# First modulation blocks loaded together; four column blocks of FFN 1 in plain products

## The chip, the cores and the metric

The kernel runs on 1 core of a Trainium2 chip. The metric is device time in microseconds for one execution. Engines are named as the profile names them: PE (TensorE matmul), PEld (its weight load), DVE (VectorE), ACT (ScalarE), POOL (GpSimd) and SP (SyncE, which issues the DMAs here).

## The reference

One layer, D = 1024, 512 latent tokens (`x`) and 256 context tokens (`xc`). Cut to what the change touches:

```
x = x + grid_pos_embedding
m  = split(silu(c)     @ w_mod + b_mod, 9)      # modulation of the latents
mc = split(silu(c_ctx) @ w_mod + b_mod, 9)      # of the context
h  = rmsnorm(x, g_n1) * (1 + m[1]) + m[0]
x  = x  + 0.5 * m[2]  * swiglu(h,  w_ffn1_up, w_ffn1_down)     # FFN 1, hidden 2816
xc = xc + 0.5 * mc[2] * swiglu(hc, w_ffn1_up, w_ffn1_down)
...                                                            # mixers on rmsnorm(x), rmsnorm(xc)
x  = x + m[5] * (merged @ w_out)
x  = x + 0.5 * m[8] * swiglu(mod(rmsnorm(x)), w_ffn2_up, w_ffn2_down)
y  = rmsnorm(x, g_final)
swiglu(x): g, u = split(x @ w_up); (silu(g) * u) @ w_down
```

## The kernel before

Features lie on the partitions: `x` is 8 feature blocks of 128 x 512, `xc` 8 of 128 x 256. Every f32 operand and weight is split into a high part (ACT, `split`, L146) and a low part (DVE, L147), and each product takes three matmuls: high weight by high operand, high by low, low by high. A Tile scheduler fixes each engine's order at build time.

**Start.** `mod_first(k)` (L198) makes m[0] and m[1] of feature block k: it loads 1 MB of weights through the rotating `raw` buffers (4 of 128x1024, `wload`, L149), runs 8 matmuls of 256 columns (L203), transposes the result on DVE (L206) and adds the bias in 8 small additions (L211). Blocks 0 to 4 stand ahead of the norm, blocks 5 to 7 inside `hook1`, between the norm and the FFN. The norm sums squares of `x` and `xc` (ACT L277, DVE L279), two matmuls with ones add them up (L283), and the reciprocal roots `rs` and `rsc` follow on ACT and DVE (L303 to L309). Each feature block is then scaled on DVE (`xr`, L617 and L618) and modulated on ACT (L632).

**FFN 1** runs over 22 column blocks of w_up (each 128 gate columns with their 128 up columns), in groups of 4, 4, 4, 4, 2, 4; after each group the matching rows of w_down are applied (L173 to L177 with operand `H`, then L560 and L562 into `x` and `xc`). The 768 tokens are cut into two halves of 384 columns and the 8 feature blocks into pairs. An up block is computed by seven block products in place of eight (`UpBlock`, `product`, L425 to L427): 7 x 4 x 3 = 84 matmuls of 384 columns. For that, DVE forms sums of weights (`UpWeights.b`, L393 to L398) and, once, sums of operands (`Operands.sums`, L356 to L359), and afterwards combines the products (L466 to L483). Four products need sums of operands. Three pairs of split weights are buffered (`whi`, `wlo`, WB = 3).

**Beside it** `more_mods` computes the other modulation parts on DVE, two products with 128x1024 weights per step (L234); m[2] has to be there when the first w_down is applied.

**The output projection** (`run_parts`, 8 blocks of w_out, first over tokens 0 to 255, then over 256 to 511) loads and splits each block of w_out in both passes.

Of the kernel before, what the change touches and what calls it, by code (L numbers as in the profile page):

```python
# [48 lines left out]
GRID_W = 64  # L49
UW = 2 + CTX + 4 + SEQ + 1  # L50
# [17 lines left out]
def block_kernel(ctx: ExitStack, tc: tile.TileContext, io):  # L68
# [110 lines left out]
    def both(t, k):  # L179
        return [t[0][:, k], t[1][:, k]]  # L180
# [4 lines left out]
    nhs, nls = (nhc, nh), (nlc, nl)  # L185
# [11 lines left out]

    def mod_first(k):  # L198
        ps = psum_small()
        raw = wload(io["wmod01"][k], 2048)  # L200
        last["mod"] = last["load"]
        for i in range(KB):
            T.matmul(ps[:, :256], c32[:, i, :], raw[i // 4][:, (i % 4) * 256:(i % 4 + 1) * 256],  # L203
                     start=(i == 0), stop=(i == KB - 1))
        tt = A.tile([P, 256], F32, name="tt", bufs=2)
        V.transpose(tt, ps[:, :256])  # L206
        tv = tt.rearrange("p (B q r) -> p B q r", B=2, q=4)
        for q in range(4):
# [9 lines left out]
    M[0], M[1] = mod_tile(0), mod_tile(1)  # L218
# [107 lines left out]
    class Operands:  # L326
# [36 lines left out]
        WHERE = {1: ("b1", 0), 2: ("b2", 0), 3: ("b2", 1), 4: ("tb", 1), 5: ("tb", 0), 6: ("ta", 0), 7: ("ta", 1)}  # L363

# [121 lines left out]
    def ffn(reg, up, downs, gate, two, ops, begin, parts, between):  # L486
# [3 lines left out]
        sel = (lambda t, k: [t[:, k, :CTX], t[:, k, CTX:]]) if two else (lambda t, k: [t[:, k]])  # L490
        x = X[0]
        groups = GROUPS[two]
        ahead = 1 if two else 2
        ws = [UpWeights(reg, up[f]) for f in range(FB)]
        f0 = 0
        blocks_ = [UpBlock(u, ops) for u in ws]
        for f in range(ahead):
            ws[f].a()
# [17 lines left out]
        for gi, gs in enumerate(groups):  # L516
            hs = reg[0].tile([P, 2 * HMAX[two] * w], F32R, name="H")
            hh, hl = (hs[:, i * HMAX[two] * w:(i * HMAX[two] + gs) * w].rearrange("p (k n) -> p k n", k=gs)
                      for i in range(2))
            for i in range(gs):  # L520
                f = f0 + i
                if i < gs - 1:
                    ws[f + 1].load()
# [6 lines left out]
                split(u, hh[:, i], hl[:, i])  # L530
# [21 lines left out]
            if gi < len(groups) - 1:  # L552
                for d in range(KB):
# [4 lines left out]
                    for k in range(gs):  # L558
                        mm(ps, wt, k, sel(hh, k), sel(hl, k), k == 0, k == gs - 1)
# [4 lines left out]
            else:  # L564
                between(100)
                run_parts(parts, weights if two else weights_held, gs, lambda k, c: (hh[:, k, c], hl[:, k, c]), g)
# [48 lines left out]
    xr = A.tile([P, KB * ALL], F32, name="xr", tag="H").rearrange("p (k n) -> p k n", k=KB)  # L615
    for k in range(KB):
# [8 lines left out]
    def hook1():  # L625
        for k in range(KB):
            if k > 4:
                mod_first(k)
# [470 lines left out]
```

## Time and profile before

| | |
|---|---|
| median of 3 runs | 1515.37 us (1514.85 to 1519.92) |
| the profiled execution's own time | 1515.29 us |
| its span | 1513.5 us |
| mean granted TensorE clock | 0.983 |
| PE, DVE, ACT busy | 94%, 84%, 48% of the span |

Read the profile by stretches: the shares of the whole span hide that the first 70 us differ from all that follows. A row of a timeline gives start, duration, engine, line, operation, output and input; brackets give the idle time ahead and what ended it. Times of PE's single matmuls overlap, so the distance of two starts is the pace, not the duration.

### The profile page before, as it was taken

To read this page: it belongs to the slowest core of one execution; us is meant where nothing else is said; L and a number is where in the kernel's file an instruction comes from. 1 tells how busy PE (TensorE), PEld (TensorE's weight loads), DVE (VectorE), ACT (ScalarE), POOL (GpSimd) and SP (SyncE) were. 2 spreads that over 40 slices of the span, in tenths; PEclk is the share of its full clock that TensorE was granted. 3 is DMA by queue.
4 is the path that set the end of the run, shared out by engine and by line. 5 is a ranking of instruction groups with operands and counts; after the bars stand their busy time and mean duration, and the time that the engine had idled before them with its cause. 6 is when DMAs were issued, how large, how long until landed. Compare 5 with 4: busy or idle time off the path is not lost.

```text
span 1513.5 us, 20675 instructions
## 1 busy us (share of the span) xinstructions
PE 1429.8 (94%) x8094; PEld 1280.4 (85%) x8094; DVE 1265.9 (84%) x1957; ACT 730.6 (48%) x1011; POOL 11.4 (1%) x55
## 2 busy tenths in 40 slices
PE   6599999999999999999999989999996999999997
PEld 5498898989988997787788768778896989999897
DVE  6998998876768868999999999966589968678686
ACT  4642341423313345578888862246366525435252
POOL 0000000000000000000000020000000000000000
PEclk9899999999999999999999999999997999999998
DMA  7435444351425134222222223233351333333331
GB/s 283 139 114 171 153 147 150 118 185 55 159 93 181 57 98 147 77 67 74 75 72 91 71 63 94 80 112 141 109 169 56 98 112 98 99 99 96 112 98 56
DMA packets 49346, 169.02 MB, mean 112 GB/s; under 512 B 5600, under 2 KB 7904, under 8 KB 48608
## 3 DMA queue, kind: packets, MB, share of 16 engines
q1 hardware_dynamic: 49248, 167.70, 34.2%
q8 instruction: 63, 1.03, 0.3%
q14 instruction: 35, 0.29, 0.1%
HBM read 163.48 MB, written 4.19 MB: 111 GB/s over the span
## 4 chain that ended last, share of the span: by engine, by line
PE 63%; DVE 24%; DMA 7%; issue 3%; ACT 3%; DVEq 0%; SPq 0%; ACTq 0%
PE psm L177 11%; PE psm L175 11%; PE psm L173 11%; PE psm L425 9%; PE psm L426 8%; PE psm L427 8%; DVE wlo L147 5%; DMA raw<-in_wmod 4%; DVE cv L742 3%; DMA raw<-in_down 2%; ACT whi L146 1%; PE psm L203 1%; DVE raw L234 1%; PE ps L175 1%; PE ps L173 1%
## 5 line engine op out<-in xcount | busy, mean ns | idle before, releaser
L146 ACT ACTIVATE whi<-raw 128x1024 fp32r<-128x1024 f32 (+2 forms) x230 | 233.2, 1014 | 356.7 <-PE psm L175 235.9
L147 DVE TENSOR_TENSOR wlo<-raw,whi 128x1024 fp32r<-128x1024 f32 (+2 forms) x230 | 267.5, 1164 | 38.7 <-ACT whi L146 38.4
L742 DVE SCALAR_TENSOR_TENSOR cv<-u,vec,cv 128x512 f32<-128x512 f32 x236 | 165.2, 743 | 0.5
L173 PE MATMUL psm<-H,whi 128*128 128x256 f32 (+1 forms) x496 | 151.2, 354 | 4.2 <-ACT H L146 4.2
L175 PE MATMUL psm<-H,whi 128*128 128x256 f32 (+1 forms) x496 | 151.4, 353 | 0.0
L177 PE MATMUL psm<-H,wlo 128*128 128x256 f32 (+1 forms) x496 | 150.6, 352 | 0.0
L173 PE MATMUL psm<-nh,whi 128*128 128x512 f32 x336 | 133.0, 398 | 6.9 <-ACT u L724 2.8
L177 PE MATMUL psm<-nh,wlo 128*128 128x512 f32 x336 | 132.6, 395 | 3.6 <-DVE wlo L147 3.6
L175 PE MATMUL psm<-nl,whi 128*128 128x512 f32 x336 | 133.0, 396 | 1.7 <-DVE nl L317 1.5
L425 PE MATMUL psm<-nbx,whi 128*128 128x384 f32 x286 | 97.6, 342 | 14.6 <-ACT nbx L146 8.2
L173 PEld LDWEIGHTS psm<-H,whi 128*128 128x128 f32 x496 | 92.5, 188 | 18.4 <-ACT H L146 5.7
L175 PEld LDWEIGHTS psm<-H,whi 128*128 128x128 f32 x496 | 92.9, 188 | 13.7 <-DVE H L147 0.7
L177 PEld LDWEIGHTS psm<-H,wlo 128*128 128x128 f32 x496 | 93.2, 188 | 12.9
L426 PE MATMUL psm<-nbx,whi 128*128 128x384 f32 x286 | 97.2, 340 | 0.9 <-DVE nbx L147 0.9
L427 PE MATMUL psm<-nbx,wlo 128*128 128x384 f32 x286 | 96.5, 340 | 0.4 <-DVE wlo L147 0.3
L425 PE MATMUL psm<-nb,whi 128*128 128x256 f32 x264 | 77.3, 294 | 10.1 <-ACT nb L146 9.2
L234 DVE SCALAR_TENSOR_TENSOR raw<-raw,cb 128x1024 f32<-128x1024 f32 x56 | 68.2, 1219 | 18.2 <-DMA raw<-in_wmod 18.1
L173 PEld LDWEIGHTS psm<-nh,whi 128*128 128x128 f32 x336 | 63.9, 191 | 21.6 <-ACT u L724 3.1
L426 PE MATMUL psm<-nl,whi 128*128 128x256 f32 (+1 forms) x264 | 79.9, 303 | 0.0
L560 DVE SCALAR_TENSOR_TENSOR x<-psm,m,x 128x512 f32<-128x512 f32 x64 | 47.8, 746 | 38.4 <-PE psm L177 38.4
L146 ACT ACTIVATE whi<-s 128x1024 fp32r<-128x1024 f32 x44 | 46.7, 1062 | 68.0 <-PE psm L426 24.5
L177 PEld LDWEIGHTS psm<-nh,wlo 128*128 128x128 f32 x336 | 64.0, 191 | 18.1 <-DVE wlo L147 4.6
(296 smaller groups left out, 3772.9 us busy)
## 6 DMA issues: line engine op xcount, KB each, us to landing
raw<-in_up SPq DMA_DIRECT2D x88, 512.0 KB, 3.8
raw<-in_wmod SPq DMA_DIRECT2D x72, 512.0 KB, 4.1
raw<-in_down SPq DMA_DIRECT2D x30, 512.0 KB, 4.0
raw<-in_down SPq DMA_DIRECT2D x24, 384.0 KB, 3.3
raw<-in_wvg SPq DMA_DIRECT2D x16, 512.0 KB, 3.8
raw<-in_wout SPq DMA_DIRECT2D x16, 512.0 KB, 4.0
raw<-in_wlx SPq DMA_DIRECT2D x10, 512.0 KB, 3.8
raw<-in_wlg SPq DMA_DIRECT2D x10, 512.0 KB, 3.7
```

The source lines that it names most:

```text
L146: S.activation(hi, src, AF.Copy)
L147: V.tensor_tensor(lo, src, f32(hi), op=ALU.subtract)
L173: T.matmul(p_, hi[:, wk, :], h, start=first, stop=False)
L175: T.matmul(p_, hi[:, wk, :], l, start=False, stop=False)
L177: T.matmul(p_, lo[:, wk, :], h, start=False, stop=last)
L203: T.matmul(ps[:, :256], c32[:, i, :], raw[i // 4][:, (i % 4) * 256:(i % 4 + 1) * 256], start=(i == 0), stop=(i == KB - 1))
L234: V.scalar_tensor_tensor(o, raw, 1.0, cb[j], op0=ALU.mult, op1=ALU.mult, accum_out=out[:, j:j + 1])
L425: T.matmul(ps, hi[:, o + k, :], h, start=first and k == 0, stop=False, **kw)
L426: T.matmul(ps, hi[:, o + k, :], l, start=False, stop=False, **kw)
L427: T.matmul(ps, lo[:, o + k, :], h, start=False, stop=k == 3, **kw)
L560: V.scalar_tensor_tensor(x[:, d], ps[-1], g[:, d, 0:1], x[:, d], op0=ALU.mult, op1=ALU.add)
L742: V.scalar_tensor_tensor(o, u[:, t:t + SEQ], wdw[:, j, t:t + 1], o, op0=ALU.mult, op1=ALU.add)
```

## The change

- The 8 MB of weights of `mod_first` get space of their own, in tiles that hold later operands (`nh`, `nbx`, two context tiles). All loads are issued at once, among those of `x` and `xc`; five matmul groups run ahead of the norm's end, three inside `hook1`. The bias is added for both parts in one instruction (4 in place of 8 per block).
- The weights of the first two up blocks are loaded early, too.
- The first group of FFN 1 (4 up blocks) is computed in eight plain block products (`PlainBlock`): 8 x 4 x 3 = 96 matmuls of 384 columns per block, no sums of weights, no combinations afterwards. Its first block goes by feature block: as soon as feature block k is split, its 12 matmuls are issued. The sums of operands that later groups need are made one pair per plain block (`sums1`).
- `H` is four tiles in place of one.
- In the output projection the split weights of blocks 3 to 7 are kept for the second pass (40 KB per partition), so that it loads and splits three in place of eight.

```
+    def mod_load(k, dst):
+        at[k] = dst
+        for a in range(0, 2048, 1024):
+            last["mod"] = nc.sync.dma_start(dst[:, a:a + 1024], io["wmod01"][k][:, a:a + 1024])
...
     def mod_first(k):
         ps = psum_small()
-        raw = wload(io["wmod01"][k], 2048)
...
+            T.matmul(ps[:, :256], c32[:, i, :], at[k][:, i * 256:(i + 1) * 256], start=(i == 0), stop=(i == KB - 1))
...
+    class PlainBlock:
...
+        def step(self, kk, start, stop):
+            if self.ps is None:
+                self.ps = [[psum_small()[:, :self.nw] for _ in range(2)] for _ in range(2)]
+            i, half = kk // 2, kk % 2
+            b = [self.ops.plain(half, c, i) for c in range(2)]
+            for wt, ps in zip(self.wt, self.ps):
+                mm(ps, wt, kk, [h for h, _ in b], [l for _, l in b], start, stop, wk=half * 4 + i)
...
         if two:
-            begin()
-            ws[0].b()
-            ws[0].c()
-            ws[0].d()
+            for p_ in plain[:2]:
+                p_.load()
+            plain[0].prepare()
+            begin(lambda kk: plain[0].step(kk, kk == 0, kk == KB - 1))
...
+                if f < len(plain):
+                    if f + 1 < len(plain):
+                        plain[f + 1].prepare()
...
+                    if f:
+                        plain[f].all()
+                    u = plain[f].post()
+                    sums(f)
...
-    mod_first(0)
+    mod_load(0, spare[0])
+    mod_load(1, spare[1])
     nc.sync.dma_start(pos, io["pos"])
     nc.sync.dma_start(x[:, :4], io["x"][:, :4])
-    mod_first(1)
     nc.sync.dma_start(x[:, 4:], io["x"][:, 4:])
+    mod_load(2, spare[2])
     nc.sync.dma_start(xc, io["xc"])
-    for k in range(2, 5):
+    first_up = [UpWeights([A], io["up1"][f]) for f in range(2)]
+    for k in range(3, KB):
+        mod_load(k, spare[k])
+        if k in (4, 7):
+            first_up[k == 7].load()
+    for k in range(MA):
         mod_first(k)
...
+    def hook1(step):
...
         for k in range(KB):
-            if k > 4:
-                mod_first(k)
+            if k + MA < KB:
+                mod_first(k + MA)
+            if k + 1 < KB:
+                scale_x(k + 1)
...
+            step(k)
...
+    def out_weights(d, key):
+        if d in held:
+            return held[d]
```

SP, from its start: before, each line with `raw` waits for a free one of the four buffers.

```order
L154 DMA raw<-in_wmod 128x1024 x2
L595 DMA pos<-in_pos 128x288
L596 DMA x<-in_x 128x2048
L154 DMA raw<-in_wmod 128x1024 x2
L598 DMA x<-in_x 128x2048
L599 DMA xc<-in_xc 128x2048
L154 DMA raw<-in_wmod 128x1024 x6
L154 DMA raw<-in_up 128x1024 x2
L154 DMA raw<-in_wmod 128x1024 x6
```

SP, the same place after; `mod` is the new space, which nothing holds yet.

```order
L204 DMA mod_72<-in_wmod 128x1024 x4
L666 DMA pos<-in_pos 128x288
L667 DMA x<-in_x 128x2048
L668 DMA x<-in_x 128x2048
L204 DMA mod_101<-in_wmod 128x1024 x2
L670 DMA xc<-in_xc 128x2048
L204 DMA mod_101<-in_wmod 128x1024 x4
L158 DMA raw<-in_up 128x1024 x2
L204 DMA mod_101<-in_wmod 128x1024 x2
L204 DMA mod_77<-in_wmod 128x1024 x2
L204 DMA mod_78<-in_wmod 128x1024 x2
L158 DMA raw<-in_up 128x1024 x2
```

Both halves of `x` and one more modulation block now stand ahead of `xc`, and all eight modulation blocks are issued without a wait.

PE, from its start, before (`psm<-raw` are the modulation matmuls, L425 to L427 the first products of FFN 1):

```order
L203 MATMUL psm<-raw,c_95 128x256 x33
L283 MATMUL psm<-acc,ones 128x512
L283 MATMUL psm<-accc,ones 128x256
L203 MATMUL psm<-raw,c_95 128x256 x27
L425 MATMUL psm<-nhc,whi 128x384
L203 MATMUL psm<-raw,c_95 128x256 x4
L426 MATMUL psm<-nlc,whi 128x384
L427 MATMUL psm<-nhc,wlo 128x384
```

PE after, the same place (L177 to L181 are the plain products, `nl` and `p` their operands of feature block 0):

```order
L209 MATMUL psm<-mod_72,c_95 128x256 x16
L209 MATMUL psm<-mod_101,c_95 128x256 x22
L290 MATMUL psm<-acc,ones 128x512
L290 MATMUL psm<-accc,ones 128x256
L209 MATMUL psm<-mod_101,c_95 128x256 x10
L177 MATMUL psm<-nl,whi 128x384
L177 MATMUL psm<-p_299,whi 128x384
L177 MATMUL psm<-nl,whi 128x384
L177 MATMUL psm<-p_299,whi 128x384
L209 MATMUL psm<-mod_77,c_95 128x256 x2
L179 MATMUL psm<-nl,whi 128x384
L181 MATMUL psm<-nl,wlo 128x384
```

The first FFN product now follows 48 modulation matmuls in place of 60 and is followed by further products of the same feature block. From the second w_down stage of FFN 1 up to the output projection, and from FFN 2's first products to the end, the instructions of PE and DVE stand in the same order before and after, but for two matmuls that change places.

## Rows read from the trace of the kernel before

**Rows 1.** Stretches: length, then busy us (count) by engine, PE clock, DMA share, GB/s.
```profile
0.00:6.00 6.00, 0.16 (x1) 0.20 (x2) 1.11 (x2) 1.50 (x2) 0.48 (x7) 1.00 0.61 174
6.00:21.00 15.00, 11.39 (x42) 9.34 (x43) 10.21 (x34) 4.55 (x10) 0.16 (x2) 1.00 1.02 417
...
51.00:66.00 15.00, 4.41 (x15) 2.54 (x13) 13.82 (x46) 11.98 (x18) 0.00 (x0) 0.73 0.25 82
...
68.50:128.50 60.00, 58.75 (x320) 57.27 (x321) 56.16 (x85) 23.72 (x35) 0.00 (x0) 0.97 0.39 126
128.50:163.20 34.70, 33.86 (x194) 29.57 (x193) 31.31 (x56) 7.15 (x9) 0.00 (x0) 1.00 0.50 161
```

**Rows 2.** Chain of waits: start, us, what; the last modulation block.
```profile
49.80 2.01 PE psm L203 x8
```

**Rows 3.** PE's timeline: two paces, w_down of the first group, the next up block.
```profile
68.98 0.52 PE L425 MATMUL psm<-nbx,whi 128*128 128x384 f32 x1
69.30 0.52 PE L426 MATMUL psm<-nbx,whi 128*128 128x384 f32 x1
...
75.10 0.33 PE L425 MATMUL psm<-nl,whi 128*128 128x384 f32 x1
75.27 0.33 PE L426 MATMUL psm<-nl,whi 128*128 128x384 f32 x1
...
128.59 0.51 PE L173 MATMUL psm<-H,whi 128*128 128x256 f32 x2
...
163.23 0.33 PE L425 MATMUL psm<-nhc,whi 128*128 128x384 f32 x1
...
167.58 0.44 PE L425 MATMUL psm<-nbx,whi 128*128 128x384 f32 x1 [2.10 <-ACT whi L146]
```

**Rows 4.** DVE's groups, 0 to 70 us: count, busy us, mean ns, idle ahead.
```profile
L147 DVE TENSOR_TENSOR nh<-xr,nh 128x768 fp32r<-128x768 f32 x2 | 1.9, 952 | 0.0
L147 DVE TENSOR_TENSOR nbx<-xr,nbx 128x384 fp32r<-128x384 f32 x3 | 1.7, 554 | 0.3 <-ACT nbx L146 0.3
...
L393 DVE TENSOR_TENSOR s<-raw 128x512 f32<-128x512 f32 x1 | 0.7, 691 | 1.7 <-DMA raw<-in_up 1.7
```

**Rows 5.** ACT's groups, 0 to 70 us, in the same columns.
```profile
L632 ACT ACTIVATE xr<-xr,m,G 128x512 f32<-128x512 f32 x8 | 6.4, 802 | 3.4 <-DVE xr L617 3.4
L632 ACT ACTIVATE xr<-xr,m,G 128x256 f32<-128x256 f32 x8 | 4.7, 592 | 3.0 <-DVE G L263 2.4 <-DVE xr L618 0.5
...
L146 ACT ACTIVATE nbx<-t 128x768 fp32r<-128x768 f32 x5 | 4.2, 835 | 0.5 <-DVE t L359 0.5
...
L228 ACT ACTIVATE cb<-cb 128x1024 f32<-128x1024 f32 x2 | 2.1, 1058 | 1.5 <-DMA cb<-in_cc 1.5
...
L146 ACT ACTIVATE nbx<-xr 128x384 fp32r<-128x384 f32 x3 | 1.5, 508 | 0.0
...
L228 ACT ACT_TABLE_LOAD x1 | 1.3, 1283 | 0.0
```

**Rows 6.** Timeline of DVE and ACT around the norm and the first scaled feature blocks.
```profile
17.45 0.42 ACT L275 ACTIVATE accc<-xc 128x256 f32<-128x256 f32 x1 [5.52 <-DMA xc<-in_xc]
...
33.67 0.65 DVE L617 TENSOR_TENSOR xr<-x,rs 128x512 f32<-128x512 f32 x1
...
36.27 0.52 ACT L146 ACTIVATE nhc<-xr 128x384 fp32r<-128x384 f32 x1
...
37.40 0.68 DVE L617 TENSOR_TENSOR xr<-x,rs 128x512 f32<-128x512 f32 x1
38.00 0.42 DVE L618 TENSOR_TENSOR xr<-xc,rsc 128x256 f32<-128x256 f32 x1
```

**Rows 7.** DVE's groups, 68.5 to 128.5 us, in the columns of Rows 4.
```profile
L147 DVE TENSOR_TENSOR wlo<-raw,whi 128x1024 fp32r<-128x1024 f32 x8 | 9.8, 1221 | 2.5 <-ACT whi L146 2.5
```

**Rows 8.** Stretches late in the run, in the columns of Rows 1.
```profile
1120.00:1130.00 10.00, 10.00 (x85) 10.00 (x84) 10.00 (x22) 9.82 (x22) 0.00 (x0) 1.00 0.49 166
...
1150.00:1160.00 10.00, 8.30 (x29) 6.82 (x30) 9.37 (x21) 6.45 (x12) 0.00 (x0) 0.50 0.13 45
```

More of the change, by code (lines that the diff above doesn't have):

```diff
@@ L363, in block_kernel, with plain @@
         WHERE = {1: ("b1", 0), 2: ("b2", 0), 3: ("b2", 1), 4: ("tb", 1), 5: ("tb", 0), 6: ("ta", 0), 7: ("ta", 1)}
+        def plain(self, half, c, k):
+            tag, o = (("b1", 0), ("b12", 0), ("b2", 0), ("b2", 1))[half * 2 + c]
+            return [t[:, o * self.nw:(o + 1) * self.nw] for t in self.parts[tag, k]]
         def of(self, p, k):
@@ L484, in rest, with __init__, load, prepare @@
             return u
-    def ffn(reg, up, downs, gate, two, ops, begin, parts, between):
+    class PlainBlock:
+        def __init__(self, w, ops):
+            self.w, self.ops, self.nw, self.ps = w, ops, ops.nw, None
+        def load(self):
+            self.w.load()
+        def prepare(self):
+            self.load()
+            self.wt = [self.w.pair(r) for r in self.w.raw]
+        def step(self, kk, start, stop):
[5 more added lines that the diff above has]
+                mm(ps, wt, kk, [h for h, _ in b], [l for _, l in b], start, stop, wk=half * 4 + i)
+        def all(self):
+            order = [2 * i + h for h in range(2) for i in range(4)]
+            for kk in order:
+                self.step(kk, kk == order[0], kk == order[-1])
+        def post(self):
+            nw = self.nw
+            g, u = tmp(2 * nw), tmp(2 * nw)
+            for c in range(2):
+                o = slice(c * nw, c * nw + nw)
+                S.activation(g[:, o], self.ps[0][c], AF.Silu)
+            for c in range(2):
+                o = slice(c * nw, c * nw + nw)
+                V.tensor_tensor(u[:, o], self.ps[1][c], g[:, o], op=ALU.mult)
+            return u
@@ L489, in ffn @@
+    def ffn(reg, up, downs, gate, two, ops, begin, parts, between, sums=None):
         w = ALL if two else SEQ
-        sel = (lambda t, k: [t[:, k, :CTX], t[:, k, CTX:]]) if two else (lambda t, k: [t[:, k]])
+        sel = (lambda t: [t[:, :CTX], t[:, CTX:]]) if two else (lambda t: [t])
         x = X[0]
         groups = GROUPS[two]
-        ahead = 1 if two else 2
-        ws = [UpWeights(reg, up[f]) for f in range(FB)]
+        ahead = 0 if two else 2
+        ws = (first_up if two else []) + [UpWeights(reg, up[f]) for f in range(2 if two else 0, FB)]
@@ L565, in ffn @@
                 between(100)
[L566 removed]
+                run_parts(parts, weights if two else weights_held, gs, lambda k, c, hs=hs: (hs[k][:, 0, c], hs[k][:, 1, c]), g)
             f0 += gs
@@ L621, in block_kernel, with scale_x @@
+    def scale_x(k):
+        V.tensor_tensor(xr[k][:, CTX:], x[:, k], rs1, op=ALU.mult)
+        V.tensor_tensor(xr[k][:, :CTX], xc[:, k], rs1c, op=ALU.mult)
+    scale_x(0)
     flat = "p k n -> p (k n)"
     ops1 = Operands(ALL // 2)
-    ops1.place([t.rearrange(flat) for t in (nh, nl, nhc, nlc)] + [nbx], b2=2, ta=2, tb=2, b1=1)
-    def hook1():
+    tiles = {}
+    def hook1(step):
+        plain = Operands(ALL // 2)
+        plain.add([A.tile([P, 1024], F32R, name="p21", tag="s21"), A.tile([P, 512], F32R, name="p4", tag="s4")]
+                  + [A.tile([P, 512], F32R, name=f"p4{t}", tag=f"w4{t}") for t in "hl"]
+                  + [keep("acc", SEQ, F32R), keep("rs", SEQ, F32R), A.tile([P, 384], F32R, name="p0")])
+        plain.place(b12=1)
+        ops1.parts.update(plain.parts)
+        nw = ALL // 2
```

109 lines of the change are left out of this document (73 added, 36 removed).

## The prediction

> **What bounds the kernel now.** I read the busy time by stretches first, then PE's own timeline, then the groups of DVE and ACT in the first 70 us. From 68.5 us on PE is the engine that sets the pace: in the 60 us of the first four up blocks it is busy for 58.75 us, in the following w_down stage for 33.86 of 34.70 us [rows 1]. DVE is close behind (56.16 and 31.31 us), so a change there has to keep both in view. Before 68.5 us PE has little to do: between 51 and 66 us it is busy for 4.41 of 15 us, at a mean granted clock of 0.73 [rows 1]. Two things hold it up there, one after the other. The modulation blocks come through four buffers, so the last is multiplied only at 49.80 us and is done at 51.81 [rows 2], although the transfers ran at 417 GB/s between 6 and 21 us [rows 1]. Then DVE and ACT split the operands and their sums, and only when these are nearly through do the seven-product blocks run without gaps. The marks of the run before: 68.5 us (dense matmuls begin; 16 of the first block's 84 are through), 128.59 (first w_down), 163.23 (next up block) [rows 3].
>
> **The loads.** The 417 GB/s were reached with several transfers in flight [rows 1]; I take that rate for the new order, in which nothing waits for a buffer, and that data land in the order of issue. By 6 us 1.04 MB are in (174 GB/s [rows 1]), and so come: `x` complete (4.4 MB) at 14 us, `xc` (6.5 MB) at 19.1, modulation block 4 (8.6 MB) at 24, the first up weights at 26.6, modulation block 7 (12.8 MB) at 34, the second up weights at 36.7. So modulation leaves the path: by the DVE sum below its turn comes at about 48 us. `xc` comes 1.65 us later than the 17.45 of before [rows 6], since a modulation block stands ahead of it now. Against that, DVE stood for 1.7 us on the first up weights in the middle of the root chain [rows 4]; these now land before it. I set the two off: first `xr` at 33.7 us as before, first split operand at 36.8 us as before [rows 6]. Bounds: 1.7 us either way.
>
> *A rule weighed.* The Trainium skill (DMA: Bandwidth & Descriptors, Bandwidth) sets reads from device memory at about 358 GB/s per core; the trace differs with its 417 GB/s, and the measurement decides here. By the page `xc` would land some 2 us later, and the sum would be 2 us longer.
>
> **The first block, by feature block.** Three engines work side by side from 34 to 60 us, and the last of them decides. Neighbouring instructions of DVE overlap by 0.08 us (a 0.68 us addition is followed after 0.60) [rows 6]; I take that off on DVE and 0.1 us on ACT.
> - DVE: eight `xr` pairs at 0.94 us, 7.5 [rows 6]; low parts, eight of 384 columns at 0.47 and four of 768 at 0.87, 7.2 [rows 4]; two weight splits at 1.14 and one modulation product, taken as long as a split of its width, 3.4 [rows 7]; three transposes and twelve small bias additions, 2.5 by estimate from the 0.42 us of a 256-wide addition [rows 6]. Sum 20.6, from 33.7: 54.3 us.
> - ACT: eight modulated blocks at 0.70 + 0.49, 9.5; high parts, eight at 0.41 and four at 0.74, 6.2; three operations of 1024 columns at 0.96, 2.9; one table load, 1.3 [rows 5]. Sum 19.9, from 34.4: 54.3 us.
> - Each hands over to the other some ten times. Their groups stood between 0 and 3.4 us for such waits [rows 4, 5]; I add 2.5 in all (0 to 6). Last low part 57 us, and with the rest of the last feature block's matmuls 59 us.
> - PE: 96 matmuls at 0.174 (75.10 to 75.27 [rows 3]), 16.7; two modulation blocks at 2.01 [rows 2], 4.0; from 36.8: 57.5 us. PE stands for about 5 us before this, and the dense work of before began at the lower clock after its gaps: 0.32 us per matmul from 68.98 to 69.30, 0.174 at 75.10 [rows 3], so up to 6 us at half pace. I take 5 us, 2.5 us lost (0 to 3): 60.0 us.
>
> So block 1 of the group can begin at **60 us** (57 to 65).
>
> **The other three plain blocks.** 3 x 96 x 0.174 = 50.1 us. Per block this is 2.1 us more PE time than the 84 matmuls of before; it is what the change pays. DVE's work per block is two weight splits (2.3), two multiplications out of PSUM (0.9), one pair's sums (1.9 + 1.7), one low part of `H` (0.9) and four modulation products (4.6, by their width again): 12.3 us [rows 4, 7], under PE's 16.7. The two weight splits are the narrow place: with three buffers the second pair of the next block can only be split when the block before has read its first pair for the last time. From there PE has 12 matmuls (2.1 us) to the first use of the new high part and 16 (2.8 us) to its low part; ACT and DVE need 1.06 and 1.22 us [rows 5, 7], together 2.3. It fits if DVE is free at that moment, and costs up to 1.1 us where a modulation product is in front. I take 1.0 us in all (0 to 7). First w_down at 60 + 50.1 + 1 = **111.1 us**, 17.5 before the 128.59 of now.
>
> **w_down and the next up block.** The 192 matmuls of w_down are the same, 34.6 us (163.23 - 128.59): next up block at 145.7. There PE waited 2.10 us for split weights, which come from DVE's sums [rows 3]. DVE's backlog is smaller now: each plain block leaves out four weight additions (0.61 each [rows 4]), one and a half weight splits and three to four combinations, some 6 us, 24 in all, while PE comes 17.5 earlier. So that wait should go: -2 us (0 to -2.4). From there on the order of PE and DVE is what it was, and both come earlier by at least as much, so what is gained here stays. Single `H` tiles are freed at nearly the same moment as before: 0.
>
> **Output projection.** The second pass saves five splits, 5.7 us of DVE and 5 us of ACT [rows 5, 7]. But PE was busy through all of it (10.00 of 10 us between 1120 and 1130 [rows 8]), and the freed time stands ahead of nothing that PE waits for; the order behind it is unchanged. In the first pass three splits now stand ahead of the last merged operand. Value 0, bounds -1 and +1.
>
> **Sum.** 1515.3 - 17.5 - 2 = 1495.8; against its own time of 1515.29, which is the median within 0.1 us.
>
> **Rivals.**
> 1. *The weight splits set the pace of the plain blocks.* Each of the three boundaries, and the start of w_down, waits for the full chain of 2.3 us, and handing over in the first block costs 3 us more: 4 x 2.3 + 3 = 12 us less gain at most, 1507.5; with half of it 1502. For it: DVE is busy for 56 of 60 us here already [rows 1], and wlo waited 2.5 us for ACT [rows 7]. Against it: DVE's sum of 12.3 in 16.7 us.
> 2. *The loads do not land in order.* If all transfers in flight share the engines, `x` and `xc` come with the last blocks near 34 us. The norm then starts 15 us later, and so does block 1 (75 us): 1515.3 - 19.5 + 15 = 1511. For it: `xc` already took 12.5 us from 5 to 17.45 with less in flight [rows 6]. Against it: that is what 6 MB need in order.
>    The Trainium skill (DMA: Bandwidth & Descriptors, Queues, rings and completion order) says that each DMA engine takes one issuer's descriptors in ring order; by that rule this rival falls.
> 3. *The clock stays at its lower level* (slower). The first block is fed in eight portions with gaps, and gaps of about a microsecond between the plain blocks could keep PE at 1.2 of 2.4 GHz: between 1150 and 1160 us the granted clock was 0.50 though PE was busy for 8.30 of 10 us [rows 8]. A matmul then takes 0.32 in place of 0.174, a modulation block 4.0 in place of 2.0. (a) In the first block alone PE needs 96 x 0.32 + 8 = 38.7 us, block 1 begins at 75.5, 15.5 later: 1511. (b) In all four: 15.5 + 288 x 0.146 = 57.5 more, 1553. The change turns into a loss from 134 slow matmuls on (19.5 / 0.146). Against it: at half pace PE has the operands waiting, so the first block has no gaps then, and after 68.5 us dense work brought 0.174 back [rows 3]; the last three blocks have all operands at hand.
>    The Trainium skill (TensorE: Matmul & The Clock Gate, HAM oscillation) tells of a kernel whose bursts between waits each ran at the lower clock; by that rule (a) is the least that this change would pay.
> 4. *Everything fits*: no start at the lower clock, no wait at boundaries, 57 us for block 1: 1515.3 - 21.5 - 2.4 = 1491, at best 1487.
>
> **How the numbers follow.** The forecast (1489 to 1501, with rival 4 in it) has 0.62. Rival 1 (1501 to 1507.5) has 0.16, rival 2 0.07 and rival 3a 0.04 (both within 0.5%, 7.6 us, which is about what a measurement of this kernel can tell from no change), rival 3b 0.06, a still larger gain (under 1489) 0.05. Faster 0.83, the same 0.11, slower 0.06. The range takes in the forecast's bounds and most of rival 1: 1488 to 1506.
>
> **What would show it.** In the profile after: the last modulation matmul near 46 us in place of 51.8; the first plain product near 37; 96 matmuls of block 1 ended near 60; PE without gaps over 1 us up to w_down, near 111 us, clock 1.00 from about 42 us; the next up block near 144 with no wait at its third product; the rest shifted by one constant. Wrong would be: `rs` later than 35 us (rival 2), PE waiting for `whi` or `wlo` at each block's second weights (rival 1), a clock of 0.50 past 60 us (rival 3), or a shift that shrinks between 145 us and the end, which no step here foresees.

## The result and the profile after

The changed kernel takes 1498.03 us (median; 1496.73 to 1501.72) against 1517.64 us of the kernel before in the same comparison: a ratio of 0.9875, with a 95% interval from 0.9846 to 0.9905. Its profiled execution took 1496.73 us (span 1494.9) against 1515.29 us before, so 18.6 us less; by the medians it is 19.6 us less. The prediction was 1495.8 us, 19.5 us less than the 1515.3 us of before.

The busy times of the whole run stand first on the page (share of the span, count of instructions):

```profile
PE 1431.8 (96%) x8142; PEld 1287.4 (86%) x8142; DVE 1234.0 (83%) x1884; ACT 716.4 (48%) x994; POOL 11.4 (1%) x55
```

PE has 48 matmul records more than before and works 2 us longer (1429.8 before); DVE works 32 us less (1265.9 before). The time was gained because PE starts its dense work earlier, not because it has less to do. By stretches, in the columns of [rows 1] (length, busy us and count by engine, granted clock, DMA share, GB/s):

```profile
6.00:21.00 15.00, 13.79 (x48) 11.05 (x48) 6.91 (x19) 1.33 (x3) 0.00 (x0) 1.00 1.01 405
21.00:36.00 15.00, 12.15 (x52) 9.71 (x52) 14.10 (x41) 12.00 (x23) 0.00 (x0) 1.00 1.03 416
36.00:51.00 15.00, 12.23 (x54) 11.22 (x55) 13.81 (x34) 13.14 (x20) 0.00 (x0) 0.89 0.36 138
51.00:64.00 13.00, 13.00 (x76) 12.92 (x75) 8.82 (x20) 8.67 (x15) 0.00 (x0) 1.00 0.37 122
64.00:114.00 50.00, 50.00 (x289) 49.85 (x288) 45.14 (x75) 17.23 (x25) 0.00 (x0) 1.00 0.47 152
114.20:148.60 34.40, 33.66 (x194) 29.52 (x193) 33.41 (x55) 9.40 (x11) 0.00 (x0) 1.00 0.43 138
```

From 51 to 64 us PE is now busy all the time (before, it was busy for 4.41 of the 15 us from 51 to 66 [rows 1]), and it does not pause once in the 50 us of the three further plain blocks. PE's timeline gives the marks that answer to [rows 3] (start, us, line, operation, tiles; in brackets the idle time ahead and what ended it):

```profile
38.77 0.45 PE L177 MATMUL psm<-nl,whi 128*128 128x384 f32 x1 [3.25 <-ACT nl L150]
39.05 0.34 PE L177 MATMUL psm<-p,whi 128*128 128x384 f32 x1
39.23 0.34 PE L177 MATMUL psm<-nl,whi 128*128 128x384 f32 x1
...
42.22 0.52 PE L181 MATMUL psm<-p,wlo 128*128 128x384 f32 x1
42.54 0.52 PE L179 MATMUL psm<-nl,whi 128*128 128x384 f32 x1
...
43.11 0.34 PE L181 MATMUL psm<-nl,wlo 128*128 128x384 f32 x1
43.28 0.34 PE L181 MATMUL psm<-p,wlo 128*128 128x384 f32 x1
...
48.16 3.62 PE L209 MATMUL psm<-mod,c 128*128 128x256 f32 x16
51.42 0.53 PE L177 MATMUL psm<-nh,whi 128*128 128x384 f32 x1
...
64.13 0.33 PE L177 MATMUL psm<-nl,whi 128*128 128x384 f32 x1
...
65.17 0.34 PE L177 MATMUL psm<-nl,whi 128*128 128x384 f32 x1
...
65.87 0.34 PE L181 MATMUL psm<-nl,wlo 128*128 128x384 f32 x1
...
114.25 0.51 PE L177 MATMUL psm<-H,whi 128*128 128x256 f32 x2
```

The first plain product stands at 38.77 us, block 1 of the group at 64.13, the first w_down at 114.25 (before 128.59). The gain then stands as follows; each pair is the start of the same instruction in the two traces. "End of FFN 1" is the product with ones for the next norm, in the last w_down stage.

| mark | before | after | difference |
|---|---|---|---|
| first w_down | 128.59 | 114.25 | -14.34 |
| next up block | 163.23 | 148.64 | -14.59 |
| second w_down | 225.61 | 208.26 | -17.35 |
| end of FFN 1 | 582.00 | 564.57 | -17.43 |
| output projection begins | 1088.10 | 1069.43 | -18.67 |
| first waiting product of FFN 2 | 1146.32 | 1127.46 | -18.86 |
| ones product of the final norm | 1503.40 | 1484.79 | -18.61 |

Nearly all of it is there by 208 us. A second trace of the same changed kernel (after_again below) has its marks up to 0.8 us away from these (63.88, 114.00, 209.00 and 563.93 us), so smaller differences between single traces say little. What follows asks which of the parts of the change brought it, and what keeps block 1 from beginning earlier.

### The profile page after: what moved, and what is told of

Same layout as the page of the kernel before. It is cut to its first block, busy times and chain, and to the rows that moved or that the text cites. A ratio compares the mean times of both kernels' runs of the same rounds, so it can differ in the third digit from the quotient of the medians.

```text
span 1494.9 us, 20659 instructions
## 1 busy us (share of the span) xinstructions
PE 1431.8 (96%) x8142; PEld 1287.4 (86%) x8142; DVE 1234.0 (83%) x1884; ACT 716.4 (48%) x994; POOL 11.4 (1%) x55
## 3 DMA queue, kind: packets, MB, share of 16 engines
q8 instruction: 63, 1.03, 0.3%
## 4 chain that ended last, share of the span: by engine, by line
PE 69%; DVE 21%; DMA 5%; issue 3%; ACT 2%; DVEq 0%; SPq 0%; ACTq 0%
PE psm L177 13%; PE psm L181 13%; PE psm L179 13%; PE psm L444 8%; PE psm L446 8%; PE psm L445 8%; DVE wlo L151 4%; DVE cv L849 3%; DMA raw<-in_wmod 2%; DMA raw<-in_up 1%; PE psm L209 1%; PE ps L179 1%; DVE raw L241 1%; PE ps L177 1%; PE ps L181 1%
## 5 line engine op out<-in xcount | busy, mean ns | idle before, releaser
L150 ACT ACTIVATE whi<-raw 128x1024 fp32r<-128x1024 f32 (+2 forms) x220 | 222.6, 1013 | 339.0 <-PE psm L179 244.3
L151 DVE TENSOR_TENSOR wlo<-raw,whi 128x1024 fp32r<-128x1024 f32 (+2 forms) x220 | 256.1, 1165 | 31.1 <-ACT whi L150 30.8
L177 PE MATMUL psm<-H,whi 128*128 128x256 f32 (+1 forms) x496 | 150.8, 354 | 2.9 <-ACT H L150 2.9
L181 PE MATMUL psm<-H,wlo 128*128 128x256 f32 (+1 forms) x496 | 150.8, 352 | 0.0
L177 PE MATMUL psm<-nh,whi 128*128 128x512 f32 (+1 forms) x368 | 143.0, 394 | 6.6 <-ACT u L831 2.7
L179 PE MATMUL psm<-nl,whi 128*128 128x512 f32 (+1 forms) x376 | 144.8, 392 | 1.7 <-DVE nl L324 1.5
L181 PE MATMUL psm<-nh,wlo 128*128 128x512 f32 (+1 forms) x368 | 142.2, 390 | 2.0 <-DVE wlo L151 2.0
L177 PEld LDWEIGHTS psm<-H,whi 128*128 128x128 f32 x496 | 92.3, 188 | 17.1 <-ACT H L150 4.1
L179 PEld LDWEIGHTS psm<-H,whi 128*128 128x128 f32 x496 | 92.9, 188 | 13.4 <-DVE H L151 0.4
L181 PEld LDWEIGHTS psm<-H,wlo 128*128 128x128 f32 x496 | 93.1, 188 | 12.8
L444 PE MATMUL psm<-nbx,whi 128*128 128x384 f32 x252 | 85.5, 339 | 4.7 <-DVE t L493 3.2
L444 PE MATMUL psm<-nb,whi 128*128 128x256 f32 x264 | 77.4, 295 | 12.1 <-ACT nb L150 10.9
L177 PEld LDWEIGHTS psm<-nh,whi 128*128 128x128 f32 x368 | 69.9, 191 | 21.5 <-ACT u L831 3.0
L179 PEld LDWEIGHTS psm<-nl,whi 128*128 128x128 f32 x376 | 71.8, 192 | 17.1 <-DVE nl L324 3.0
L446 PE MATMUL psm<-nbx,wlo 128*128 128x384 f32 x252 | 84.6, 336 | 0.0
L241 DVE SCALAR_TENSOR_TENSOR raw<-raw,cb 128x1024 f32<-128x1024 f32 x56 | 68.4, 1221 | 19.5 <-DMA raw<-in_wmod 19.2
L181 PEld LDWEIGHTS psm<-nh,wlo 128*128 128x128 f32 x368 | 69.9, 190 | 16.6 <-DVE wlo L151 3.0
L445 PE MATMUL psm<-nb,whi 128*128 128x256 f32 x264 | 76.3, 289 | 0.0
```

Of the source, the lines that this page charges most:

```text
L150: S.activation(hi, src, AF.Copy)
L151: V.tensor_tensor(lo, src, f32(hi), op=ALU.subtract)
L177: T.matmul(p_, hi[:, wk, :], h, start=first, stop=False)
L179: T.matmul(p_, hi[:, wk, :], l, start=False, stop=False)
L181: T.matmul(p_, lo[:, wk, :], h, start=False, stop=last)
L241: V.scalar_tensor_tensor(o, raw, 1.0, cb[j], op0=ALU.mult, op1=ALU.mult, accum_out=out[:, j:j + 1])
```

## The experiments

Two theories stood against each other. **A**: the start was held by DVE and ACT (operands and their sums), so the plain blocks bring the gain and the early loads little. **B**: it was held by the modulation blocks' late loads. The marks of all kernels, from the trace of each, with the ratio to the kernel before on the same chip (its medians there were 1517.21, 1518.41 and 1517.38 us):

| kernel | median us | ratio, 95% | block 1 | first w_down | end of FFN 1 |
|---|---|---|---|---|---|
| after | 1498.03 | 0.9875 (0.9846 to 0.9905) | 64.13 | 114.25 | 564.57 |
| e_loads | 1516.36 | 0.9989 (0.9975 to 1.0004) | - | 128.92 | 584.26 |
| e_rot | 1502.78 | 0.9900 (0.9881 to 0.9919) | 66.31 | 118.73 | 567.82 |
| e_nohold | 1495.53 | 0.9859 (0.9838 to 0.9880) | 63.40 | 113.51 | 563.98 |
| e_modahead | 1496.45 | 0.9867 (0.9846 to 0.9888) | 63.09 | 113.20 | 564.41 |
| e_npl1 | 1508.94 | 0.9946 (0.9926 to 0.9966) | 64.99 | 123.71 | 574.95 |
| e_cblate | 1497.07 | 0.9876 (0.9851 to 0.9902) | 64.59 | 114.69 | 566.34 |
| e_xfirst | 1495.59 | 0.9868 (0.9844 to 0.9892) | 62.02 | 112.13 | 564.58 |
| e_best | 1495.30 | 0.9866 (0.9837 to 0.9896) | 61.12 | 112.73 | 561.47 |
| e_v4 | 1492.82 | 0.9843 (0.9828 to 0.9859) | 60.96 | 111.08 | 560.62 |
| e_npl3s | 1501.39 | 0.9890 (0.9871 to 0.9910) | 64.16 | 112.92 (see there) | 567.90 |
| after_again | 1495.71 | 0.9859 (0.9846 to 0.9873) | 63.88 | 114.00 | 563.93 |

**The early loads alone** (the kernel before, with the loads of the change; no plain block). The edit also puts the matmuls of the last three modulation blocks ahead of the operands; cut:

```
+def mod_load(k, dst):  ...
-    raw = wload(io["wmod01"][k], 2048)
+first_up = [UpWeights([A], io["up1"][f]) for f in range(2)]
+for k in range(3, KB):
+    mod_load(k, spare[k])
```

> Early loads alone: the modulation blocks in space of their own and the loads in the new order, but the seven-product blocks from the start as before (no plain blocks, w_out loaded twice as before). Theory A (operands): before, DVE was busy nearly without a gap from 30.8 us to the dense matmuls at 68.5 with operands and their sums, so the loads alone bring little: dense matmuls from 64 to 68 us, first w_down at 124 to 129 (128.59 before), time 0 to 5 us under before, 1510 to 1516. Theory B (loads): the last modulation block at 51.8 us held the start, so the loads alone bring most of the 19 us: first w_down at 112 to 117, time 1497 to 1502.

Measured: no gain (0.9989), first w_down at 128.92 us. The stretch that was idle before is idle still, now without any load in it, and PE's timeline names who is late:

```profile
51.00:66.00 15.00, 3.74 (x8) 1.76 (x8) 15.00 (x29) 12.60 (x20) 0.00 (x0) 0.50 0.00 1
```
```profile
57.94 0.69 PE L432 MATMUL psm<-nbx,whi 128*128 128x384 f32 x1 [6.76 <-ACT nbx L149]
```

DVE is busy for 15.00 of the 15 us. The wait for modulation at 49.80 us [rows 2] lay beside DVE's work, so taking it away uncovered nothing: theory A for this half. The lower clock (0.50 in this stretch) comes on top.

**The plain blocks alone** (the changed kernel with the rotating loads of before; the first up weights are not loaded early either; cut):

```
 def mod_first(k):
+    raw = wload(io["wmod01"][k], 2048)
-for k in range(3, KB):
-    mod_load(k, spare[k])
```

> Plain blocks alone: all of the change, but the modulation blocks come through the four rotating buffers in the old order of loads. After, the last modulation matmul ended at 51.4 us although all its data had landed by about 35 us; before at 51.8. Theory A (operands, PE's own queue): almost nothing is lost, block 1 begins at 63 to 67 us (64.1 after), time 0 to 3 us above after, 1497 to 1501. Theory B (loads): modulation is back on the path, block 1 begins at 70 us or later, time at least 6 us above after, 1504 or more.

Measured: 9.9 us earlier at the first w_down than before and 14.2 us earlier at the end of FFN 1. The loads now add the rest, 4.5 us at w_down and 3.25 at the end of FFN 1, although they are worth nothing alone. Of the 4.5 us, 2.2 are there at block 1 (66.31 us), since PE stood behind a late modulation block; most of the rest is two waits for split weights that arrive late in the plain blocks, 0.86 and 1.01 us:

```profile
36.84 5.41 PE L207 MATMUL psm<-raw,c 128*128 128x256 f32 x16 [3.94 <-DMA raw<-in_wmod]
...
85.73 0.45 PE L177 MATMUL psm<-nl,wlo 128*128 128x384 f32 x1 [0.86 <-DVE wlo L147]
```

So the two parts are not additive: the loads come to the front once DVE's sums are out of the way. That is more than theory A allowed for (0 to 3 us; by the medians it is 4.8), and B falls with e_loads.

**Only one plain block, and only three.** The list of sums that each plain block covers is set with it (cut):

```
+SUMS = {1: ((0, 1, 2, 3),), 3: ((0, 1), (2, 3), ()), 4: ((0,), (1,), (2,), (3,))}[NPL]
-plain = [PlainBlock(ws[f], ops) for f in range(groups[0])] if two else []
+plain = [PlainBlock(ws[f], ops) for f in range(NPL)] if two else []
-sums(f)
+for j in SUMS[f]:
+    sums(j)
```

> All of the change, but only the first up block is a plain one (by feature block); blocks 1 to 3 take seven products again, and all four pairs of sums of operands are made while PE stands at the first block's end. Theory (the plain blocks are a cover for DVE's sums): block 1 has product 1 (2.1 us) to run, then PE waits for four pairs of sums at about 3.6 us of DVE each, 12 to 16 us less what it saves, 3 x 2.1 = 6.3 us on PE: first w_down at 120 to 125 (114.25 after), time 6 to 10 us above after, 1503 to 1508. Rival (the first block by feature block is all that counts): no stall, 6 us gained, first w_down at 108, time 1491 to 1493.

> All of the change, but three plain blocks in place of four; the fourth takes seven products, its sums of weights lie in the space that holds the plain blocks' operands. Theory: PE saves 2.1 us, but the sums of weights (four additions of 0.6 us, two splits with their hand-over, 3 to 5 us) can only start when the third block has read its operands, with one product (2.1 us) to cover them, and DVE gets four additions, a split and four combinations more: first w_down at 113 to 117 (114.25 after), within 3 us of after in all. Rival (the fourth plain block is simply too many): 2 us gained, first w_down at 112.

Measured with one: 10.4 us of the gain at the end of FFN 1 is gone. All sums now stand between block 0 and a block that needs them, and PE waits again (5.98 us, then 1.27, 0.65, 0.34). Behind the first wait the granted clock is 0.50 from 73 to 85 us, and products come 0.32 us apart; the run does not tell what the waits and what the clock cost by themselves:

```profile
73.22 1.01 PE L446 MATMUL psm<-nbx,whi 128*128 128x384 f32 x2 [5.98 <-ACT nbx L152]
```
```profile
73.00:85.00 12.00, 9.27 (x22) 6.38 (x23) 12.00 (x21) 5.87 (x9) 0.00 (x0) 0.50 0.00 1
```

Measured with three: w_down begins 1.3 us earlier than in the changed kernel, and the end of FFN 1 comes 3.3 us later. (One matmul of w_down, at 110.28 us, stands ahead of the block's last product; the others begin at 112.92.) At the next up block the gain is 1.4 us, which is less than the 2.1 us of the twelve matmuls saved:

```profile
110.28 0.28 PE L179 MATMUL psm<-H,whi 128*128 128x256 f32 x1
110.73 0.44 PE L446 MATMUL psm<-nbx,whi 128*128 128x384 f32 x1 [0.17 <-DVE t L495]
...
112.92 0.39 PE L179 MATMUL psm<-H,whi 128*128 128x512 f32 x1
```

Without the fourth plain block DVE has the work back that it was spared. The wait of the kernel before at the next up block's third product [rows 3] returns, and behind it products come 0.32 us apart for some 3 us:

```profile
152.12 0.67 PE L446 MATMUL psm<-nbx,whi 128*128 128x384 f32 x1 [2.59 <-ACT whi L152]
```
```profile
152.00:156.00 4.00, 3.88 (x13) 3.75 (x14) 4.00 (x6) 1.91 (x4) 0.00 (x0) 0.57 0.84 238
```

From the next up block to the second w_down (210.57 us) this kernel loses 3.7 us against the changed one: the wait, and some ten products at the lower clock, 1.5 us by their distances (an estimate). So the plain blocks do two things: they cover the sums, and they spare DVE splits whose lack is felt as far as the second w_down. By PE's matmuls alone the fourth one would have counted as a loss of 2.1 us.

**Without the splits held over for the output projection.**

```
-HELD = 5
+HELD = 0
```

> All of the change, but no split weights of w_out kept: all eight blocks are loaded and split in both passes, as before. Theory (PE sets the pace there, the freed DVE and ACT time stands ahead of nothing): no change, profiled span 1494 to 1496.5 against 1494.9, the distance from the first matmul of the output projection to the first of FFN 2 behind its wait within 0.3 us of 58.0. Rival (DVE decides there): 1 to 5 us longer.

Measured: the stretch from the start of the output projection to the first waiting product of FFN 2 takes 57.97 us, 58.03 in the changed kernel and 58.22 before. Holding the splits is worth nothing to PE, as predicted (value 0).

**What holds block 1.** Three edits take away one suspected wait each, and a fourth is all three together (cut): the last modulation blocks go ahead of the first plain product (e_modahead), the activations of the modulation vector go behind the last operand split (e_cblate), `x` and `xc` are loaded ahead of modulation blocks 1 and 2 and `x` is added first on DVE (e_xfirst, two edits in one), and e_best.

```
 def hook1():
+    for k in range(MA, KB):
+        mod_first(k)
     for k in range(KB):
-        if k + MA < KB:
-            mod_first(k + MA)
```
```
-                ops1.put("b2", k // 2, b)
+                last["exp"] = ops1.put("b2", k // 2, b)
```
```
-mod_load(1, spare[1])
 nc.sync.dma_start(pos, io["pos"])
 ...
-mod_load(2, spare[2])
 nc.sync.dma_start(xc, io["xc"])
+mod_load(1, spare[1])
+mod_load(2, spare[2])
-for k in range(MA):
-    mod_first(k)
 ...
+for k in range(MA):
+    mod_first(k)
```

> All of the change, but the matmuls of modulation blocks 5 to 7 stand ahead of the first plain product in place of among the first products. After, PE stood 3.25 us before the first plain product at 38.77, ran at half pace to 43, and was then contiguous to 64.1, with two modulation blocks of 3.3 us in between. Theory (PE's own work and the clock after the gap set block 1): the gap is filled, no slow stretch, first product at 41 to 43, block 1 at 61 to 62.5 us (limited then by the last low part, 59 to 60, plus 2.1), span 1.6 to 3 us under after, 1492 to 1493.3. Rival (the hand-overs of DVE and ACT set it): block 1 at 64, no gain. Other rival: a later first product is simply lost, block 1 at 66 to 67.

> All of the change, but the two activations of the modulation input for the DVE products (table load and 2 x 1.06 us of ACT, and behind them 1.04 us of waiting and 1.23 us of DVE ahead of the last low part) stand behind the last feature block's split instead of in the middle. Theory (PE was contiguous from 38.77 to 64.1, so PE's own work sets block 1): the last low part ends 2 to 3 us earlier, at 57 to 58, but block 1 still begins at 63.5 to 64.5 and the time stays within 1 us of after. Rival (ACT and DVE set it): block 1 at 61 to 62, 2 to 3 us gained.

> All of the change, but pos, x and xc are issued right behind modulation block 0, ahead of the other seven, and the additions to x stand ahead of the modulation matmuls' transpositions in the program. Theory (the late xc, 20.90 us, and DVE standing 10 us for the transposition set the norm): xc at 14 to 15 us, ones matmul at 26 to 28 in place of 29.7, first scaled block at 32 to 34 in place of 35.86, first product at 35 to 37, block 1 at 61 to 62.5, span 1.5 to 3 us under after. Rival (the modulation blocks, now later, hold PE instead): block 1 at 64 or later.

> The three edits together: x and xc early, modulation blocks 5 to 7 ahead of the first product, the two activations behind the last split. Theory: ones at 26 to 28, first product at 40 to 41.5 (31 modulation matmuls of 0.41 us behind the ones), no gap and no slow stretch, the last low part under 56, block 1 at 57 to 59 by PE's own work (16.7 us), first w_down at 107 to 109, 5 to 7 us under after, 1490 to 1492. Rival (gaps move elsewhere, or the clock drops again at the first product): block 1 at 61 or later, 0 to 3 us.

Measured, block 1 against 64.13 us: e_modahead -1.0, e_cblate +0.5, e_xfirst -2.1, e_best -3.0. The order of the loads and additions helps most. The two traces show why: in the kernel before, DVE's additions of `x` begin as soon as its first half has landed, and in the changed kernel that half is issued behind two modulation blocks in place of one, at 3.96 us, and lands 9.5 us later, at 13.4. The transposition of modulation block 0 also stands ahead of the additions there, but by itself it costs 0.8 us at most (before, then after):

```profile
9.97 1.29 DVE L609 TENSOR_TENSOR x<-x,pos 128x512 f32<-128x512 f32 x2 [6.86 <-DMA x<-in_x]
```
```profile
3.96 0.72 SPq L667 DMA_DIRECT2D x<-in_x  x1
```
```profile
13.01 0.45 DVE L211 STREAM_TRANSPOSE tt<-psm 128x256 f32<-128x256 f32 x1 [9.96 <-PE psm L209]
...
14.27 1.29 DVE L685 TENSOR_TENSOR x<-x,pos 128x512 f32<-128x512 f32 x2
...
35.86 0.69 DVE L697 TENSOR_TENSOR xr<-x,rs 128x512 f32<-128x512 f32 x1
```

In e_xfirst the additions begin at 10.10 us, and DVE's last sum of squares begins at 22.25. Yet the ones product that needs it begins at 28.92, since four modulation blocks stand ahead of it in PE's list and the second one's load lands later now (PE stands until 16.34 us); so the first `xr` moves by 1.15 us only, to 34.71:

```profile
10.10 2.50 DVE L683 TENSOR_TENSOR x<-x,pos 128x512 f32<-128x512 f32 x4 [7.02 <-DMA x<-in_x]
...
22.25 0.42 DVE L286 TENSOR_TENSOR accc<-accc,t 128x256 f32<-128x256 f32 x1
...
34.71 0.65 DVE L697 TENSOR_TENSOR xr<-x,rs 128x512 f32<-128x512 f32 x1
```
```profile
28.92 1.02 PE L290 MATMUL psm<-acc,ones 128*128 128x512 f32 x2
```

The other two edits mostly shift a wait. With the modulation blocks ahead PE waits for DVE's operands, 0.95 and 0.58 us (51.85 and 53.29 us), and then the granted clock falls, which costs some 1.5 us more (an estimate from the distances of the products, 0.32 us from 54.24 to 56.80):

```profile
53.00:57.00 4.00, 3.71 (x12) 3.46 (x13) 2.69 (x5) 4.00 (x8) 0.00 (x0) 0.57 0.40 131
```

In e_best PE waits behind the last operand for the low part of the next weights; the activations of the modulation vector, now behind the last operand, are a likely cause:

```profile
64.23 0.44 PE L182 MATMUL psm<-nl,wlo 128*128 128x384 f32 x1 [1.22 <-DVE wlo L151]
```

In the changed kernel PE's list takes 25.4 us from its first product to block 1, and DVE's takes 24.2 us from the first `xr` to the last low part, which PE needs 4 us before block 1. The two are nearly equal, and taking work from one alone gained a microsecond at most here.

**A version from these findings**, with the changed kernel unaltered beside it (after_again): modulation block 1 between the two halves of `x`, the others behind `xc`, the additions first, modulation block 4 behind the norm's ones products, blocks 5 to 7 ahead of the first plain product (cut).

```
 nc.sync.dma_start(x[:, :4], io["x"][:, :4])
+mod_load(1, spare[1])
 nc.sync.dma_start(x[:, 4:], io["x"][:, 4:])
 nc.sync.dma_start(xc, io["xc"])
+mod_load(2, spare[2])
 ...
+for k in range(4):
+    mod_first(k)
 ...
+for k in range(4, MA):
+    mod_first(k)
 scale_x(0)
```

> The kernel after with another start: modulation block 1 between the halves of x, then xc, then the other modulation blocks; the sums of squares and their ones matmul ahead of modulation block 4 and half of 3; modulation blocks 4 to 7 ahead of the first plain product. The two activations of the modulation input stay where they were. Theory (after the ones it is PE's own list, 31 to 40 modulation matmuls of 0.41 us and 96 of 0.174, and beside it DVE's chain of 24 us from the first scaled block): ones at 25 to 27, first scaled block at 31 to 33, block 1 at 57.5 to 60 (64.1 after), first w_down at 108 to 110.5, no new wait at the block boundaries, 4 to 6 us under after at the end of FFN 1, 1491 to 1494. Rival (DVE, 97% busy in the first groups, takes the gain back before FFN 1 ends): at most 2 us under after there.

> The kernel after, unchanged, beside the other two on the same chip, so that they can be compared with it. Expected: its ratio to before within 0.985 to 0.990; in its trace block 1 at 63.5 to 64.5, first w_down at 113.5 to 115, the shift at the end of FFN 1 within 1 us of the 17.4 found, and the stretch from there to the output projection anywhere between 503.7 and 506.4 us, as in the other runs, whose order there is the same.

Measured: 1492.82 us against 1495.71 of the changed kernel on the same chip, 2.9 us less. The intervals of the two ratios overlap by 0.0013, so the times alone do not settle it; the traces agree with it: the end of FFN 1 stands at 560.62 us against 563.93. Three modulation blocks in place of four stand ahead of the ones products, the first `xr` comes 5 us earlier (30.77), and PE goes from the ones products through the modulation blocks into the plain products without a pause:

```profile
24.90 1.10 PE L290 MATMUL psm<-acc,ones 128*128 128x512 f32 x2 [1.54 <-DVE acc L286]
25.83 0.59 PE L290 MATMUL psm<-accc,ones 128*128 128x256 f32 x2
26.26 17.00 PE L209 MATMUL psm<-mod,c 128*128 128x256 f32 x78
42.91 0.53 PE L177 MATMUL psm<-nl,whi 128*128 128x384 f32 x1
```

Block 1 begins at 60.96 us, still outside the 57.5 to 60 us that were expected: 17 us of modulation now stand ahead of the first product, so PE's own list is the limit (42.91 + 16.7 + a wait of 0.79 + some 0.5).

## Why the prediction came out right, and where its steps were off

What the change brings, and by which way, was foreseen: dense work begins earlier, and the wait behind w_down goes. That the sum came within 1 us of the profiled execution is partly luck, since a first block that came 4.1 us late met several smaller gains, 1.2 us of them in a part that the change does not touch. In the order of the prediction, measured against it:

- **The loads: right in rate, late by 2 us at the first product.** Rival 2 fell: data landed in the order of issue, at 405 and 416 GB/s against the 417 taken from [rows 1]. ACT met `xc` at 20.90 us (predicted 19.1, before 17.45 [rows 6]), the first `xr` stood at 35.86 (predicted 33.7), the first plain product at 38.77 (predicted 36.8). The step that failed is the set-off "1.7 us against 1.65": the prediction followed `xc`, but `x` came late, too. DVE's additions began 4.3 us later than before (14.27 against 9.97), for the reason shown under e_xfirst. From 16.46 us to the last sum, which ends at 29.87, DVE had no idle time, with 2.1 us for transpositions and biases of two modulation blocks in between, which before stood behind the sums. The ones product came 3.5 us later than before (29.68 against 26.18), and the root chain behind it was shorter by 1.3 us in place of 1.7. `xc` itself came 1.8 us later than predicted, although the rate was right: 175 GB/s up to 6 us and 405 from there make 7.1 MB by 20.9 us, while the loads up to `xc` are 6.5 MB, so part of the rate went to transfers behind it. Nor were the eight modulation blocks issued without a wait, as the section on the change says: SyncE issued the last six of their transfers between 18.40 and 26.17 us, each behind the landing of an earlier one; the DMA share of 1.01 and 1.03 shows that this left no idle time.

  The Trainium skill (DMA: Bandwidth & Descriptors, Bandwidth) gives about 358 GB/s for each core where both cores of a pair read from device memory; this trace, on a single working core, shows 405 to 416. Another of its pages (HBM Reference, Specifications (TRN2)) names some 425 GB/s for a core that streams alone, which the trace comes near to. So the 2 us that the prediction weighed by the 358 GB/s do not apply here.

```profile
20.90 0.42 ACT L282 ACTIVATE accc<-xc 128x256 f32<-128x256 f32 x1 [4.67 <-DMA xc<-in_xc]
```

- **The first block: predicted 60 us, measured 64.1.** The PE sum was the right one to go by; its start and one of its terms were off. The start was 2.0 us late (above). A modulation block was taken as the 2.01 us of [rows 2]; but that row is half a block. After shows 16 records in a row from 48.16 to 51.42 us, 3.26 us, and 128 records for eight blocks; so the two blocks cost 6.5 us in place of 4.0, 2.5 more. The term for the clock, 2.5 us, measured 2.1: 25.36 us from 38.77 to 64.13, less 16.7 and 6.5; PE had stood for 3.25 us ahead of it in place of 5. Together 60 + 2.0 + 2.5 - 0.4 = 64.1.
- **DVE's and ACT's sums in the first block** said 57 us for the last low part; it ended at 60.0, with the start 2 us late and 1 us of waiting for ACT's activation of the modulation vector ahead of it. PE, which did not wait, was the longer one, by little: with the modulation blocks out of its way it waits for ACT and DVE (e_modahead).

```profile
57.91 1.23 DVE L241 SCALAR_TENSOR_TENSOR junk<-raw,cb 128x1024 bf16<-128x1024 f32 x1 [1.04 <-ACT cb L235]
...
59.06 0.95 DVE L151 TENSOR_TENSOR nhc<-xr,nhc 128x768 fp32r<-128x768 f32 x1
```

- **The other three plain blocks: 50.12 us, predicted 50.1 + 1.0.** Rival 1 did not come true, by a narrow margin. The weights' splits did wait for PE to give up the buffer, as it said:

```profile
62.95 1.06 ACT L150 ACTIVATE whi<-raw 128x1024 fp32r<-128x1024 f32 x1 [4.33 <-PE psm L179]
```
```profile
64.04 1.23 DVE L151 TENSOR_TENSOR wlo<-raw,whi 128x1024 fp32r<-128x1024 f32 x1 [2.88 <-ACT whi L150]
```

  The high part was ready at 64.01 us and first used at 65.17, the low part was ready at 65.27 and first used at 65.87: 0.6 us to spare. In e_rot (0.86 and 1.01 us) and in e_best (1.22 us) that margin was gone, and PE did wait. The 5.7 us for which DVE waited on `whi` from 64 to 114 us (2.5 before [rows 7]) stayed off the path.
- **w_down: 34.39 us, predicted 34.6**, with one pause of 0.74 us for ACT's split of `H`.
- **The wait at the third product: gone.** The shift grew by 2.76 us from the next up block to the second w_down (predicted 2; 2.02 in after_again). In the answer on waits for that stretch (us in total, times, longest) PE's own entry is now 0.5 us, where before it waited 2.1, 0.3 and 0.2; e_npl3s brought the wait back:

```profile
PE psm L444 <- DVE t L493: 0.5, 1, 0.5
```
```profile
PE psm L425 <- ACT whi L146: 2.1, 1, 2.1
PE psm L427 <- DVE wlo L147: 0.3, 1, 0.3
PE psm L425 <- DVE t L474: 0.2, 1, 0.2
```

- **The clock (rival 3):** the granted clock was 0.89 from 36 to 51 us, behind the 3.25 us for which PE had stood: products came 0.18 us apart at first (39.05 to 39.23), 0.32 apart up to 42.54 us and 0.17 from 43.11 on; from 51 us on it is 1.00. The Trainium skill's account of bursts that each run at the lower clock (TensorE: Matmul & The Clock Gate, HAM oscillation) does not bear on this trace: behind the first slow products PE never waited before block 1, and no later portion of the first block ran slow.
- **Output projection: -0.19 us, predicted 0**; e_nohold shows that its edit is worth nothing.
- **The mixers: -1.24 us, not foreseen, and within the spread of the traces.** From the end of FFN 1 to the output projection the instructions of PE, DVE and ACT stand in the same order in all kernels, and they took between 503.7 and 506.3 us in the thirteen traces: 506.10 before, 504.86 after, 506.22 in e_npl1, 503.80 in e_nohold. Spells of a lower clock lie at different places in it (before, and after):

```profile
752.00:760.00 8.00, 6.41 (x25) 5.15 (x26) 8.00 (x12) 7.54 (x11) 0.16 (x2) 0.79 0.30 100
```
```profile
592.00:600.00 8.00, 6.47 (x16) 5.09 (x17) 6.36 (x16) 5.28 (x10) 0.00 (x0) 0.57 0.32 100
```

The ledger: -19.5, +4.1 (block 1), -1.0 (no waits at the boundaries), -0.2 (w_down), -0.8 (waits up to the second w_down), -0.1 (rest of FFN 1), -1.2 (mixers), -0.2 (output projection), +0.2 (FFN 2) = -18.7, against -18.6 between the two profiled executions. Which of the gaps ahead sets off a spell of the lower clock in the mixers stays open; no run here was made for it.

## What to carry to other kernels

Giving one engine more matmuls to spare another its additions can pay twice, as cover for the work in progress and as relief of the engine that falls behind later; a count of the matmuls sees neither, so follow the shift up to the point where it stays constant. Loads that wait for a buffer are worth moving only when nothing else holds the same place: take away the other cause first, then see what they bring. When a load is moved ahead, follow every load that it pushes back and the list of the engine that waits for it: here `x` came 3.5 us later for one modulation block more, and in e_xfirst, with `x` in time, PE's list still held the norm back. When a mark in a trace is to stand for a stage, look whether single instructions of the stage were put ahead of it.

## What the runs showed of the hardware

- A matmul on f32 operands of 256 columns leaves two records: 128 records for 64 of them (3.26 us for 16 records, which are the 8 matmuls of one block). The f32r products leave one. A group's count is not the program's count, and a row may hold half of what it seems to hold.
- A pause of PE could be followed by a lower clock, and not always by the same loss. Behind 3.25 us of standing, e_cblate ran products 0.32 us apart from 38.68 to 43.59 us (granted clock 0.77 from 36 to 51), the changed kernel up to 42.54 (0.89). Behind 0.95 and 0.58 us, e_modahead fell to 0.57 (53 to 57 us); behind 1.05 us at 37.91, e_xfirst stayed at 1.00 from 36 to 51. e_v4 and e_best, in which PE had no pause there, were at 1.00 in these 15 us, too (e_cblate, and e_v4):

```profile
36.00:51.00 15.00, 12.80 (x52) 11.85 (x53) 12.76 (x33) 10.33 (x17) 0.00 (x0) 0.77 0.33 132
```
```profile
36.00:51.00 15.00, 15.00 (x80) 14.15 (x79) 14.74 (x44) 11.72 (x19) 0.00 (x0) 1.00 0.46 162
```

- Such spells move a single trace by a microsecond or two: e_modahead and e_xfirst lost 1.4 and 1.3 us between 460 and 480 us (granted clock 0.91 there, 1.00 in the changed kernel), so their 1.0 and 2.1 us at block 1 had nearly vanished at the end of FFN 1. Marks close to the edit tell more than the end of one trace.
